# A hybrid attention and mLSTM layer: the gm gate projection moved between two stages, with longer chain steps and other buffer counts

## The chip, the cores and the metric

The kernel runs on one core of a Trainium2 chip, in one launch. The metric is the device time in microseconds. One profiled execution of the kernel before gives the trace from which all rows below come.

## The reference, cut to what matters

A layer has 2048 tokens of 1024 features behind 16 learned meta tokens. One input projection feeds two branches and four gates, and all of it is float32:

```python
u = _rmsnorm(h, norm_pre[layer])
proj = u @ w_in
(a_q, a_k, a_v, a_z, m_qk, m_v, m_i, m_f, m_o, m_z, g_a, g_m) = jnp.split(proj, SPLIT_POINTS, axis=-1)
att = _swa_sink_branch(a_q, a_k, a_v, sinks)      # window 128, sinks, partial rotary
y_a = (att * silu(a_z)) @ w_attn_out
m_q, m_k = split(silu(_causal_conv(m_qk, conv_w, conv_b)))
cell = _mlstm_cell(m_q, m_k, m_v, m_i, m_f)       # matrix memory, chunkwise
hm = _head_layernorm(sigmoid(m_o) * cell, head_norm)
y_m = (hm * silu(m_z)) @ w_mlstm_out
merged = sigmoid(g_a) * y_a + sigmoid(g_m) * y_m
out = h + _rmsnorm(merged @ w_out, norm_post)     # meta tokens dropped
```

The projection that the change moves is the last 1024 columns of `w_in`, those of `g_m`.

## The kernel before, in words

Each float32 operand of a matmul is split into a high and a low part of type float32r, and a product is three matmuls (high by high, high by low, low by high) that add up in one PSUM bank.

**The main stage** handles the tokens in two halves of 1024 (8 blocks of 128). In each half it goes through `PLAN`, four groups, one for each kv head and each mLSTM head. A group has an A block (`kind == "A"`: q, k and v of one kv head, 8 token tiles of 384 columns), an F block (`kind == "F"`: q and k of one mLSTM head, 4 feature tiles of 512 tokens) and an M block (`kind == "M"`: v and output gate of one mLSTM head, 8 token tiles of 512 columns). Behind the M blocks of groups 1 and 3 stands one more F block, a gate block: four feature tiles of `ga` for two token blocks of 512, 8 tiles. Every tile is 24 matmuls (8 slices of the contraction by 3), in `token_proj` or `feat_proj`. The second half repeats the plan.

TensorE's order is the order of the program; the other engines' instructions are ordered by the framework's own planner. To fill TensorE while a chain waits for other engines, the program is cut into **slots**. After every 6 matmuls of a projection, and once after every tile, `slot()` runs: a tile has 4 slots. A chain is a Python generator that puts out one step of its instructions and then yields how many slots must pass before the next step. An attention chain (`attn_block`) of a token block and kv head has five steps, separated by `ATT_YIELDS`: transposes of q and k; scores and exponentials of two heads; those of the other two and the normalised P; transposes of P, masks (`pc`, `pp`, `pmb`); the product with V (`acc`). An mLSTM chain (`mlstm_chain`) has three, separated by `ML_YIELDS`, and starts right behind its M tile.

Attention chains wait in `queue`. `slot()` starts one when `clock[0]` reaches `clock[1]` and `clock[0] % SLOTS == CHAIN_PHASE`, and the next at least `gap[0]` slots later: 12, or 8 for the last group of the second half. Buffers such as `qkv` (8) and `vt` (10) limit how many blocks may be on their way, so each tile of an A block is preceded by

```python
while len(queue) > HALF_BLOCKS - 1 - i or done[0] < total - HALF_BLOCKS + i:
    slot()
```

which runs slots without a projection between them. At the end of the stage `drain(True)` runs slots in the same way until the last chain has ended. `load_w` fetches the weights of a block in 8 slices into staging tiles (`wraw` and `wraw2`) and splits them on ScalarE (high) and VectorE (low) into `whi` and `wlo`. A gate tile leaves through `evict_f`: a tanh on ScalarE and a store to HBM.

Besides, `weight_sums` and `token_sums` build the sums of quarter matrices that the second stage needs, by DMAs from ScalarE's queue (copies) and POOL's queue (adding transfers), one every fifth slot from slot 80 on.

**The second stage** does six 1024x1024 products, az, mz, gm, att, hm and out (`MATS`), for each half of the tokens: 12 sets. A set replaces the eight products of quarter matrices by seven (`PRODS`), each of 48 matmuls of 512 columns: 336 for a set. `SETS` orders them: az, mz and gm of the first half, the same of the second half, then att, hm and out with both halves each. For each product `fetch` loads its operands, `prep` splits them (`split`, lines 963 and 964) and the matmuls of line 1142 run. Products P1 and P2 of a set begin with fresh banks. The operands `r` stay resident over sets with the same key (the tokens' operands for az, mz and gm of a half; the weights for both halves of att, hm and out): only the first set of a key loads and splits two operands per product, the others one. A finished quarter leaves through `quarter`: az and mz with a load, a tanh, several VectorE operations and stores of the operands of the later sets (`operands`), gm with one tanh and one store, hm with two loads. Loads and stores share SyncE's queue.

## Time and profile before

| | us |
|---|---|
| runs shown | 2470.49 and 2477.13, median 2473.81 |
| the profiled execution | 2478.5 |
| its span, first to last instruction | 2476.8 |
| main stage, to the last matmul of a projection | 0 to 1490 |
| second stage | 1490 to 2477 |

The profiled execution lies 4.7 us above the median. Its busy times are TensorE's matmuls 2309.2 us, weight loads 1946.3, VectorE 1591.3, ScalarE 1109.9 and POOL 595.0. A busy share over the whole span mixes both stages; the windows below part them, and each window gives the granted clock as a mean, where 1.00 is 2.4 GHz and 0.50 would be 1.2 GHz throughout.

### The profile page before, as it was taken

How to read it: one execution, taken by the hardware profiler on the slowest of the kernel's cores; microseconds unless marked ns; L12 is line 12 of the kernel's file. 1: busy time of each engine (PE TensorE's matmuls, PEld its weight loads, DVE VectorE, ACT ScalarE, POOL GpSimd, SP SyncE). 2: the span in 40 equal slices, each digit the busy share in tenths (PEclk: the TensorE clock that was granted, in tenths of full speed). 3: DMA queues.
4: the chain of work that ended last, by engine and by line, in shares of the span. 5: the costliest groups of instructions: out<-in, count | busy, mean ns of one | idle time of the engine just before them, and what ended most of it. 6: DMA issues, size and time to landing. Idle time of an engine off the chain costs nothing.

```text
span 2476.8 us, 34095 instructions
## 1 busy us (share of the span) xinstructions
PE 2309.2 (93%) x11149; PEld 1946.3 (79%) x11149; DVE 1591.3 (64%) x3435; ACT 1109.9 (45%) x2721; POOL 595.0 (24%) x1219
## 2 busy tenths in 40 slices
PE   7997899897998898999998998999999999989897
PEld 7786689787787787789887886788878888877685
DVE  7875664574766675764776855764587363666675
ACT  6543543453455454553554544434533442323442
POOL 5243344234342435434343430000000000000010
PEclk9998999998999998999999999999999999999998
DMA  6424456534567536545311118876797676889874
GB/s 227 131 54 123 113 106 117 154 91 99 124 157 226 154 103 110 123 109 130 93 47 48 47 52 269 283 223 212 234 297 229 212 252 218 286 269 305 283 262 140
DMA packets 216916, 415.53 MB, mean 168 GB/s; under 512 B 23212, under 2 KB 80896, under 8 KB 216736
## 3 DMA queue, kind: packets, MB, share of 16 engines
q1 hardware_dynamic: 200032, 352.51, 43.8%
q0 software_dynamic: 9792, 35.66, 9.9%
q10 hardware_dynamic: 6912, 25.17, 3.4%
q8 instruction: 88, 1.44, 0.2%
q14 instruction: 92, 0.75, 0.1%
HBM read 302.06 MB, written 172.00 MB: 191 GB/s over the span
## 4 chain that ended last, share of the span: by engine, by line
PE 38%; DVE 12%; DMA 10%; ACT 4%; issue 3%; POOL 2%; SPq 0%; ACTq 0%; DVEq 0%; POOLq 0%
PE x L1142 21%; PE pj L754 8%; PE pj L766 4%; DMA raw<-uo_d 3%; PE acc L519 2%; DVE xs L531 1%; DMA ld<-gm_d 1%; DVE st L964 1%; DMA wraw<-in_w_all 1%; DMA raw<-sw_d 1%; DVE r L964 1%; DVE wlo L213 1%; DVE e L1083 1%; PE s L467 1%; ACT r L963 1%
## 5 line engine op out<-in xcount | busy, mean ns | idle before, releaser
L1142 PE MATMUL x<-r,st 128*128 128x512 f32 x2688 | 623.0, 394 | 29.2 <-DVE st L964 9.5
L754 PE MATMUL pj<-whi,un 128*128 128x512 f32 (+2 forms) x1952 | 628.6, 379 | 0.1
L1142 PEld LDWEIGHTS x<-r,st 128*128 128x128 f32 x2688 | 512.2, 191 | 139.8 <-DVE st L964 10.9
L754 PEld LDWEIGHTS pj<-whi,un 128*128 128x128 f32 x1952 | 373.3, 193 | 39.7 <-issue 1.3
L754 PE MATMUL pj<-wlo,un 128*128 128x512 f32 (+2 forms) x976 | 365.2, 374 | 12.0 <-DVE wlo L213 12.0
L964 DVE TENSOR_TENSOR st<-raw,st 128x1024 fp32r<-128x1024 f32 x168 | 204.4, 1220 | 201.8 <-ACT st L963 194.4
L766 PE MATMUL pj<-un,whi 128*128 128x512 f32 x1024 | 327.7, 401 | 2.7 <-ACT xs L542 2.7
L1142 PE MATMUL x<-st,r 128*128 128x512 f32 x1344 | 309.2, 392 | 9.2 <-DVE st L964 5.3
L963 ACT CAST st<-raw 128x1024 fp32r<-128x1024 f32 x168 | 176.6, 1052 | 292.6 <-PE x L1142 158.8
L1142 PEld LDWEIGHTS x<-st,r 128*128 128x128 f32 x1344 | 253.8, 189 | 64.4 <-DVE st L964 6.0
L1050 POOL TENSOR_TENSOR yss<-yss,mhalf 128x1 f32<-128x1 f32 x16 | 12.6, 797 | 971.2 <-issue 895.2
L766 PEld LDWEIGHTS pj<-un,whi 128*128 128x128 f32 x1024 | 187.7, 191 | 38.0 <-ACT xs L542 3.1
L754 PEld LDWEIGHTS pj<-wlo,un 128*128 128x128 f32 x976 | 189.0, 194 | 34.4 <-DVE wlo L213 19.0
L766 PE MATMUL pj<-un,wlo 128*128 128x512 f32 x512 | 203.1, 397 | 0.0
L476 ACT ACTIVATE P<-s,mn 128x144 f32<-128x144 f32 x256 | 95.3, 377 | 233.2 <-DVE mn L474 200.8
L213 DVE TENSOR_TENSOR wlo<-wraw,whi 128x512 fp32r<-128x512 f32 (+3 forms) x224 | 138.7, 635 | 23.4 <-ACT whi L212 21.6
L964 DVE TENSOR_TENSOR r<-raw,r 128x1024 fp32r<-128x1024 f32 x66 | 80.5, 1222 | 96.3 <-ACT r L963 96.1
L212 ACT CAST whi<-wraw 128x512 fp32r<-128x512 f32 (+3 forms) x224 | 112.0, 530 | 41.7 <-DMA wraw<-in_w_all 27.4
L963 ACT CAST r<-raw 128x1024 fp32r<-128x1024 f32 x66 | 69.2, 1051 | 113.4 <-DMA raw<-sw_d 43.9
L766 PEld LDWEIGHTS pj<-un,wlo 128*128 128x128 f32 x512 | 97.5, 190 | 21.9
L502 POOL TENSOR_SCALAR_AFFINE_SELECT pp<-pc 128x512 fp32r<-128x512 f32 x120 | 78.7, 659 | 118.7 <-ACT pc L497 107.7
L467 PE MATMUL s<-ks,qs 128*128 128x272 f32 (+1 forms) x512 | 90.7, 298 | 15.8 <-ACT ks L448 7.5
(363 smaller groups left out, 3528.6 us busy)
## 6 DMA issues: line engine op xcount, KB each, us to landing
raw<-sw_d SPq DMA_DIRECT2D x72, 512.0 KB, 5.7
raw<-in_wq SPq DMA_DIRECT2D x54, 512.0 KB, 4.5
wraw<-in_w_all SPq DMA_DIRECT2D x96, 256.0 KB, 4.4
sw_d<-in_wq POOLq DMA_DIRECT2D x48, 512.0 KB, 7.2
raw<-uo_d SPq DMA_DIRECT2D x28, 512.0 KB, 5.4
raw<-op_att_d SPq DMA_DIRECT2D x28, 512.0 KB, 5.4
raw<-op_hm_d SPq DMA_DIRECT2D x28, 512.0 KB, 5.7
raw<-op_mg_d SPq DMA_DIRECT2D x28, 512.0 KB, 5.5
```

The source lines that it names most:

```text
L212: S.copy(hi[:, :w], raw[:, :w])
L213: tt(lo[:, :w], raw[:, :w], f(hi)[:, :w], ALU.subtract)
L467: T.matmul(sp[:, pa, c0:272], lhsT=qs[:, pr, pa, :], rhs=ks[:, i, c0:272], start=(i == 0), stop=(i == 1))
L476: S.activation(P[:, 2 * pa + pr], sp[:, pa, 128:272], AF.Exp, bias=mn[:, 2 * pr + pa:2 * pr + pa + 1], scale=-1.0, accum_out=mn[:, 4 + 2 * ...
L502: G.affine_select(pp[:, i], f(pc)[:, i], pattern=[[0, 4], [-1, 128]], compare_op=ALU.is_gt, fill=0.0, base=0, channel_multiplier=1)
L519: T.matmul(acc, lhsT=l, rhs=r.rearrange("p s q -> p (s q)"), start=(i == 0), stop=(i == len(ops) - 1))
L531: stt(acc[:, :n], raw[:, i:i + n], cw_t[:, tix, i:i + 1], acc[:, :n], ALU.mult, ALU.add)
L754: T.matmul(ps[:, :w], lhsT=us[k][:, a, o:o + 128], rhs=ww[k][:, :w], start=(n == 0), stop=(n == 3 * KT - 1))
L766: T.matmul(ps, lhsT=ww[k][:, 128 * i:128 * i + 128], rhs=us[k][:, a], start=(n == 0), stop=(n == 3 * KT - 1))
L963: S.copy(op[:, 0], raw)
L964: tt(op[:, 1], raw, f(op)[:, 0], ALU.subtract)
L1142: T.matmul(banks[bset][g], lhsT=l, rhs=r, start=(fresh and p == 0 and kk == 0 and m == 0), stop=(p == 1 and kk == 1 and m == 2), skip_grou ...
```

## The change

The matmuls of gm leave the second stage, which keeps ten sets, and come into the main stage: each half has four gate blocks, `gm` behind groups 0 and 2 and `ga` behind 1 and 3, of the same form. `gate_d["gm"]` is then written by `evict_f`. Its quarter sums fall away, and `weight_sums` takes the five matrices as two pairs and a single one. The steps of both chains stand further apart. P has two buffers, `vt` 11 instead of 10, the split weight halves 11 instead of 10, and the `wraw` staging 3 instead of 4. The `done` test of the loop is looser by one chain. The bank that takes the transposed meta part of P is no longer that of the product with V; it is a tile of its own, and `acc` is taken in the last step. The layer norm's last operation (subtract the mean, multiply) moves from VectorE to two small POOL operations and one ScalarE activation. The scratch for descriptors of POOL's DMAs is 4096 instead of 8192.

```diff
--- before.py
+++ after.py
@@ -36,8 +36,8 @@
 NHALF = NB // HALF_BLOCKS
 SBH = HALF_BLOCKS * 128 // SB
 BIG = 1e30
-ATT_YIELDS = (5, 4, 5, 5)
-ML_YIELDS = (3, 5)
+ATT_YIELDS = (5, 5, 8, 9)
+ML_YIELDS = (4, 6)
 CHAIN_PHASE = 2
 DMA_LEAD = 30
 SPLIT_LEAD = 2
@@ -76,13 +76,12 @@
         tg(i)
         fblock([("q", i), ("k", i)])
         th(i)
-        if i % 2:
-            fblock([("ga", 2 * i - 2 + j) for j in range(4)])
+        fblock([("ga" if i % 2 else "gm", 4 * (i // 2) + j) for j in range(4)])
     return plan
 
 
 PLAN = _plan()
-MATS = ("az", "mz", "gm", "att", "hm", "out")
+MATS = ("az", "mz", "att", "hm", "out")
 
 
 @with_exitstack
@@ -100,7 +99,7 @@
     dram = pool("dram", 1, DRAM)
     es1 = ExitStack()
     units = pool("units", 16, None, es1)
-    wp = pool("wp", 10, None, es1)
+    wp = pool("wp", 11, None, es1)
     stage = pool("stage", 4, None, es1)
     mconst = pool("mconst", 1, None, es1)
     ps_p = pool("ps_p", 2, PSUM, es1)
@@ -179,7 +178,7 @@
 
     def weight_sums():
         for a in range(0, len(MATS), 2):
-            pair = (a, a + 1)
+            pair = range(a, min(a + 2, len(MATS)))
             for op, i, src in ((cp, 2, (0, 0)), (cp, 0, (1, 1)), (add, 2, (0, 1)), (add, 0, (0, 1)),
                                (cp, 1, 2), (add, 1, (1, 1)), (cp, 3, 1), (add, 3, (1, 0))):
                 for m in pair:
@@ -201,7 +200,7 @@
             if seq[0] % 5 >= 3:
                 raw = extra[0].tile([128, SB], F32, name="wraw2")
             else:
-                raw = wp.tile([128, SB], F32, name="wraw", bufs=4)
+                raw = wp.tile([128, SB], F32, name="wraw", bufs=3)
             seq[0] += 1
             with (ExitStack() if first else tc.high_priority(offset=DMA_LEAD)):
                 nc.sync.dma_start(out=raw[:, :w],
@@ -427,7 +426,7 @@
             put(qkv[:, 320:384], ps[:, 256:320])
             apply_rope(qkv.rearrange("p (h d) -> p h d", d=64), b, 6, 128)
             last = b % HALF_BLOCKS == HALF_BLOCKS - 1
-            vt = vcar[g] if last and b < NB - 1 else wt("vt", [128, 2, HD], R, bufs=10)
+            vt = vcar[g] if last and b < NB - 1 else wt("vt", [128, 2, HD], R, bufs=11)
             vp = vcar[g] if b % HALF_BLOCKS == 0 else vring[0]
             vring[0] = vt
             put(vt[:, 0], ps[:, 320:384])
@@ -455,7 +454,7 @@
                 V.tensor_copy(kcar[g], f(ks)[:, :, 144:272])
             kring[0] = ks
             yield ATT_YIELDS[0]
-            P = wt("P", [128, 4, 144], bufs=1)
+            P = wt("P", [128, 4, 144], bufs=2)
             mn = wt("mn", [128, 16])
             c0 = 0 if b > 0 else 128
             for pr in range(2):
@@ -486,11 +485,10 @@
                             rv.broadcast_to([128, 2, 2, NM]), ALU.mult)
             tt(Pv[:, :, :, NM:], Pv[:, :, :, NM:], rv.broadcast_to([128, 2, 2, 128]), ALU.mult)
             yield ATT_YIELDS[2]
-            acc = ps_a.tile([128, SB], F32, name="acc")
+            tm = ps_a.tile([128, SB], F32, name="acc")
             tp = ps_t.tile([128, SB], F32, name="tr")
             for s in range(4):
                 T.transpose(out=tp[:, 128 * s:128 * s + 128], in_=P[:, s, 16:144], identity=ident_t)
-            tm = acc
             T.transpose(out=tm[0:64, 0:128], in_=Pm.rearrange("p s j -> p (s j)"), identity=ident_t)
             pc = wt("pc", [128, 2, 4, 128], R, bufs=1)
             tpv = tp.rearrange("p (s q) -> p s q", s=4)
@@ -515,6 +513,7 @@
                    (vt.rearrange("p a d -> p (a d)"), pc[:, 1])]
             if b > 0:
                 ops += [(vp.rearrange("p a d -> p (a d)"), pp[:, 0]), (vp.rearrange("p a d -> p (a d)"), pp[:, 1])]
+            acc = ps_a.tile([128, SB], F32, name="acc")
             for i, (l, r) in enumerate(ops):
                 T.matmul(acc, lhsT=l, rhs=r.rearrange("p s q -> p (s q)"), start=(i == 0), stop=(i == len(ops) - 1))
             bs = stage.tile([128, SB], F32, name="xs")[0:64]
@@ -643,7 +642,9 @@
             V.bn_aggr(sm[:, 8:10], sm[:, 2:8])
             ts(sm[:, 10:11], sm[:, 1:2], 4.0 * EPS, sm[:, 9:10], ALU.mult, ALU.add)
             G.tensor_tensor(sm[:, 11:12], sm[:, 10:11], mh_t[:, 0:1], ALU.pow)
-            ts(tho, tho, sm[:, 8:9], sm[:, 11:12], ALU.subtract, ALU.mult)
+            G.tensor_tensor(sm[:, 12:13], sm[:, 8:9], sm[:, 11:12], ALU.mult)
+            G.tensor_scalar(sm[:, 13:14], sm[:, 12:13], -1.0, 0.0, ALU.mult, ALU.add)
+            S.activation(tho, tho, AF.Identity, bias=sm[:, 13:14], scale=sm[:, 11:12])
             yield ML_YIELDS[1]
             th = ps_t.tile([128, SB], F32, name="tr")
             for i in range(2):
@@ -667,7 +668,7 @@
             rsqrt_mean(rs[:, 0], rs[:, 1], EPS)
 
         def raw_first():
-            tiles = [wt("P", [128, 4, 144], bufs=1).rearrange("p s q -> p (s q)")]
+            tiles = [wt("P", [128, 4, 144], bufs=2).rearrange("p s q -> p (s q)")]
             tiles += [wt("pmb", [128, 4, 128], bufs=1).rearrange("p s q -> p (s q)")]
             tiles += [wt("v1", [128, 2, VW], bufs=3).rearrange("p a n -> p (a n)") for _ in range(3)]
             tiles += [wt("qs", [128, 2, 2, 128], bufs=1).rearrange("p a b q -> p (a b q)")]
@@ -837,7 +838,7 @@
                     chains = []
                     for i in range(HALF_BLOCKS):
                         rs = None
-                        while len(queue) > HALF_BLOCKS - 1 - i or done[0] < total - HALF_BLOCKS + i:
+                        while len(queue) > HALF_BLOCKS - 1 - i or done[0] < total - HALF_BLOCKS + i - 1:
                             slot()
                         if c == 0 and arg == 0:
                             if i == 0:
@@ -951,7 +952,7 @@
     ring = pool("ring", 1)
     ps_1 = pool("ps_1", 4, PSUM)
     ps_0 = pool("ps_0", 4, PSUM)
-    SETS = [(n, c, ("u", c)) for c in range(NPAIR) for n in ("az", "mz", "gm")]
+    SETS = [(n, c, ("u", c)) for c in range(NPAIR) for n in ("az", "mz")]
     SETS += [(n, c, ("w", n)) for n in ("att", "hm", "out") for c in range(NPAIR)]
     OPD = {"att": "att", "hm": "hm", "out": "mg"}
     IDX = {"P1": 0, "P2": 1, "P6": 2, "P5": 3, "P7": 4, "P3": 5, "P4": 6}
@@ -1177,7 +1178,7 @@
     r["mxT"] = a["meta_tokens"].T.reshape(KT, 128, NM).transpose(1, 0, 2)
     r["gpre"] = a["norm_pre"][0].reshape(KT, 128).T
     r["w_all"] = np.concatenate([_pack(w_in, cols) for _, _, cols in PLAN])
-    mats = [w_in[:, c:c + D] for c in (C_AZ, C_MZ, C_GM)] + [a[n][0] for n in ("w_attn_out", "w_mlstm_out", "w_out")]
+    mats = [w_in[:, c:c + D] for c in (C_AZ, C_MZ)] + [a[n][0] for n in ("w_attn_out", "w_mlstm_out", "w_out")]
     r["wq"] = np.stack([m.reshape(2, 4, 128, 2, SB).transpose(0, 3, 2, 1, 4).reshape(2, 2, 128, 4 * SB) for m in mats])
     r["negs"] = a["attn_sinks"][0]
     r["cw"] = a["conv_w"][0].T.reshape(KT, 128, 4).transpose(1, 0, 2)
@@ -1204,7 +1205,7 @@
     import concourse.bacc as bacc
     from concourse.bass_utils import run_bass_kernel_spmd
 
-    nc = bacc.Bacc("TRN2", target_bir_lowering=False, num_devices=1, dynamic_dma_scratch_size=8192)
+    nc = bacc.Bacc("TRN2", target_bir_lowering=False, num_devices=1, dynamic_dma_scratch_size=4096)
     arrays, args = {}, []
     for name, a in _layout(inputs).items():
         arrays[f"in_{name}"] = a
```

## Rows read from the trace of the kernel before

**Rows 1.** The page's busy times: us, share of the span, instructions.

```profile
PE 2309.2 (93%) x11149; PEld 1946.3 (79%) x11149; DVE 1591.3 (64%) x3435; ACT 1109.9 (45%) x2721; POOL 595.0 (24%) x1219
```

**Rows 2.** Windows, both stages: length, busy by engine, clock, DMA share, GB/s.

```profile
0.00:1490.00 1490.00, 1377.42 (x7117) 1180.29 (x7117) 978.21 (x2637) 713.54 (x2178) 582.36 (x1203) 0.96 0.45 114
1490.00:2477.00 987.00, 931.79 (x4032) 765.98 (x4032) 613.10 (x798) 396.34 (x544) 12.59 (x16) 0.97 0.76 249
```

**Rows 3.** Windows: A1, A2, A3 of half 1, A1, A3 of half 2; gate block with A2.

```profile
167.00:241.00 74.00, 61.17 (x337) 56.50 (x337) 41.45 (x119) 30.17 (x117) 30.56 (x69) 0.86 0.36 104
...
401.00:445.00 44.00, 44.00 (x273) 42.77 (x272) 19.48 (x56) 17.09 (x65) 25.44 (x57) 1.00 0.50 117
548.00:622.00 74.00, 61.02 (x329) 56.23 (x328) 40.24 (x116) 28.43 (x109) 31.93 (x71) 0.86 0.43 102
928.00:992.00 64.00, 54.90 (x289) 50.45 (x288) 36.43 (x102) 26.25 (x96) 34.78 (x70) 0.87 0.66 113
...
1275.00:1335.00 60.00, 51.43 (x286) 47.70 (x285) 33.50 (x99) 25.23 (x94) 28.89 (x63) 0.94 0.10 30
...
1090.60:1183.20 92.60, 92.60 (x490) 82.91 (x490) 43.75 (x116) 36.30 (x118) 39.88 (x75) 1.00 0.56 131
```

**Rows 4.** The chain that ended last: start, length, matmuls of 384 columns.

```profile
1175.08 8.32 PE pj L754 x48
```

**Rows 5.** Windows of sets: az, mz, gm, az, gm, att, hm, out.

```profile
1498.00:1578.00 80.00, 79.36 (x336) 65.16 (x337) 55.26 (x66) 40.83 (x52) 0.00 (x0) 0.96 0.83 279
1578.00:1662.50 84.50, 79.10 (x338) 64.93 (x337) 58.77 (x83) 31.43 (x44) 0.00 (x0) 0.96 0.75 242
1662.50:1739.10 76.60, 76.47 (x338) 63.01 (x337) 39.81 (x47) 34.92 (x47) 0.00 (x0) 1.00 0.70 229
1739.10:1815.30 76.20, 76.20 (x338) 63.10 (x337) 49.58 (x62) 37.31 (x50) 0.00 (x0) 1.00 0.75 249
1898.30:1974.50 76.20, 76.20 (x337) 63.08 (x337) 40.13 (x47) 35.11 (x47) 0.00 (x0) 1.00 0.69 230
1974.50:2050.60 76.10, 76.10 (x337) 63.02 (x336) 44.08 (x50) 31.98 (x39) 0.00 (x0) 1.00 0.79 266
2204.00:2292.70 88.70, 80.31 (x338) 64.78 (x337) 64.55 (x92) 23.27 (x28) 0.00 (x0) 0.96 0.91 300
2292.70:2383.40 90.70, 80.18 (x337) 65.24 (x337) 60.71 (x82) 41.49 (x64) 2.94 (x3) 0.94 0.80 259
```

**Rows 6.** TensorE's waits, whole span: us, times, longest us.

```profile
PE acc L519 <- POOL pmb L511: 29.3, 12, 4.4
PE tr L492 <- DVE P L487: 16.8, 9, 4.6
...
PE pj L754 <- DVE wlo L213: 12.0, 13, 3.3
...
PE s L467 <- ACT P L476: 5.7, 1, 5.7
```

**Rows 7.** The same in the window 167 to 241, an A1 block.

```profile
PE acc L519 <- POOL pmb L511: 8.2, 3, 4.4
...
PE tr L492 <- DVE P L487: 1.0, 1, 1.0
```

**Rows 8.** Timeline: VectorE at the border mz to gm; TensorE in out's second product.

```profile
1670.47 0.75 DVE L1098 SCALAR_TENSOR_TENSOR bt<-ld,hn,th 128x512 f32<-128x512 f32 x1 [1.92 <-DMA op_hm_d<-bt]
...
1672.94 1.22 DVE L964 TENSOR_TENSOR st<-raw,st 128x1024 fp32r<-128x1024 f32 x1
...
2320.29 2.07 PE L1142 MATMUL x<-r,st 128*128 128x512 f32 x4 [7.34 <-DVE ld L1108]
```

**Rows 9.** VectorE's wait for POOL; POOL's small step; its transfers' time to landing.

```profile
DVE tho L646 <- POOL msm L645: 61.1, 63, 3.1
...
L645 POOL TENSOR_TENSOR msm<-msm,mhalf 128x1 f32<-128x1 f32 x64 | 37.6, 588 | 8.5 <-DVE msm L644 7.8 <-DMA kT<-in_xT 0.7
...
DMA to landing us min/median/max: 5.4/7.1/11.7
```

## The prediction, made before the change was run

> **What bounds the kernel now.** I began with the page's busy times: TensorE is busy 93% of the span, its weight loads 79%, and nothing else over 64% [rows 1]. So TensorE sets the time, and the question is which matmuls come and go and in which of its gaps. The windows by stage come next: the main stage (to 1490 us) has 112.6 us without a matmul and a granted clock of 0.96, the seven-product stage behind it 55.2 us and 0.97 [rows 2]. The change takes work out of the second and puts it into the first, so I read both by block.
>
> The main stage's lost time is not spread evenly. Its A blocks (8 token tiles of 192 matmuls in all) come in two kinds [rows 3]: A2, which follows a gate block, has no gap (44.0 us busy of 44.0), A1 and A3, which follow an M block directly, have 12.8, 13.0, 9.1 and 8.6 us of gap and a clock of 0.86 to 0.94. The code says why. A chain of attention steps may start every 12 slots and 8 are queued, 96 slots; the next A block begins 80 slots behind the last one's end if no gate block stands between, and 112 if one does. Its `while` loop then turns `slot()` with no projection beside it. Counting slots by the loops, A1 and A3 have 21, 20, 16 and 16 such bare slots, all other blocks none.
>
> In the second stage I cut the windows at each 336 matmuls, one set [rows 5]. A set without a stall takes 76.2 us. The two gm sets take 76.6 and 76.2: they are among the smooth ones. The lost time sits in mz, hm and out.
>
> **The change, part by part.** *Removed matmuls.* Two gm sets, 2 x 336, at 76.6 + 76.2: **-152.8 us** [rows 5]. With them go 28 weight loads of 512 KB, their splits, 32 tanh and 32 stores, all beside matmuls.
>
> *Added matmuls.* 4 blocks x 8 tiles x 24 = 768. Pace: 76.2/336 = 0.2268 us for 512 columns [rows 5], so **+174.2**. The Trainium skill (TensorE: Matmul & The Clock Gate, Back-to-back issue gap) gives 131 ns for such a matmul in a stream with weight loads; no row here is that fast. By it the swap would be +100.6 - 88.0 and the whole sum about 9 us lower; the row decides. The new gates' evictions, stores and weight splits are those of the ga blocks, which run without a gap (part of the 92.6 us stretch in [rows 3]), so they are hidden. If that cover failed, the nearest price is what late weight halves cost now, 12.0 us over 28 blocks [rows 6]: four more blocks, **+2** (0 to 4).
>
> *Bare slots gone.* With a gate block in every group, the same count gives 112 slots against 96 each time and, with the looser `done` test, no bare slot in any A block, although a chain grows from 19 to 27 slots. What that gives back: the 92.6 us stretch (a gate block and A2) holds 192 matmuls at 0.2268, 192 of 384 columns at 8.32/48 = 0.1733 [rows 4], and some 106 small ones in the 15.8 us left, 0.149 each [rows 3]. By these prices A1 and A3 with their x337, x329, x289 and x286 would take 54.9, 53.7, 47.8 and 47.3 us in place of 74, 74, 64 and 60 [rows 3]: **-68**. The lower bound is the gaps alone, -44; the upper is gaps plus what the lower clock takes, 0.14, 0.14, 0.13 and 0.06 of their lengths, -76. The small matmuls are not saved; they move under the gm blocks.
>
> *Longer chain steps.* They target waits of a chain on itself. TensorE waits 29.3 us for the masked block of the last step (L511), 16.8 for the normalised P, 5.7 for the exponentials of the first half [rows 6]. Of the first two, 23.8 and 6.0 are inside A1 and A3 (one of the four blocks stands in [rows 7], the others show 7.2 and 1.0, 4.2 and 2.0, 4.2 and 2.0) and are counted already. Outside them 5.5 + 10.8 + 5.7 = 22 us remain. The steps of 8 and 9 slots (before 5 and 5) add 4 us and more where the longest waits are 4.6 and 4.4; the 5.7 us one gets a single slot more, 1.4 us. I take 16 of the 22 and 4 of clock: **-20**, between 0 (the helpers' queues were late, not the step short) and -34 (all 22, and 12 of the 27 us that the lower clock takes outside A1 and A3: 0.04 x 1490 less 33). The second buffers of P, the eleventh of V and of the weight halves go with this; staging holds 11 + 3 + 2 weight tiles instead of 10 + 4 + 2, so loading looks as far ahead as before.
>
> *The layer norm's last step* moves from VectorE (27 us in all) to ScalarE behind two more POOL steps. VectorE is busy 978 of 1490 us in the main stage, ScalarE 714 [rows 2], and the step's result is used 6 slots later: 0, see the second rival.
>
> *End of the main stage.* The last group starts chains every 8 slots; the eighth now ends 5 slots after the last tile. What could be late there is L511 once, at most 4.4 us [rows 6], and five matmuls: **+3** (0 to 8). Next late behind it are the second stage's first loads.
>
> *The gm sets were also a pause.* mz is followed by gm, which loads only weights and evicts with one tanh; now az of the next half follows the first mz and att the second. Both split two operands per product instead of one. VectorE is the engine that feels it: 55.3 and 58.8 us busy in az and mz, 39.8 in gm [rows 5]. At mz to gm it waits 1.92 us for a buffer whose store has to land (1670.47), and its split for the second product comes at 1672.94, just in time [rows 8]: that border loses 0.4. Two operands put 2.4 us of splits ahead of that point and two more loads on SP's queue, behind stores that wait for VectorE. The nearest prices: az to mz loses 84.5 - 76.2 = 8.3 (busy evictions, one operand follows); hm to out 90.7 - 76.2 = 14.5 (the same evictions, two operands follow, and one 7.34 us wait for a late load [rows 5, 8]). I take 11 for each of two borders, **+22**, with ends of 1 and 29.
>
> *Weight sums.* 80 steps instead of 96, each on ACT's or POOL's queue every fifth slot, and done long before the stage ends: 0.
>
> **The sum.** Main stage 174 + 2 - 68 - 20 + 3 = +91; second stage -153 + 22 = -131; together **-40**. The profiled execution took 2478.5 us (span 2476.8), 4.7 above the median of the runs shown, so 2438 for it and **2433** on the median's scale. The ends: main stage +64 (174 + 0 - 76 - 34 + 0) and +142 (174 + 4 - 44 + 0 + 8); second stage -152 and -124; together -88 and +18. Five terms do not reach their ends at once.
>
> **The rivals.** *1. The borders cost nothing and the steps heal all.* For it: gm to az and gm to att lose nothing with two operands (76.2 and 76.1 for the sets after gm [rows 5]), so two operands alone are no load. Against: the set ahead was light there. Time: 174 + 1 - 68 - 34 + 1 - 152 = -78, 2396; anything under 2424 belongs here. Chance 0.33.
>
> *2. ScalarE waits for POOL and holds TensorE (slower).* VectorE waits for the one POOL step 61.1 us in 63 places [rows 9]. On ScalarE the wait is for three steps; at 0.59 us for each of the two new ones [rows 9] that is about 61 + 64 x 1.18 = 137 us. ScalarE empties the projection's two banks in order, so what stands behind such a wait is the next tile's eviction. If all reached TensorE: 2570. It decides against the change once 40/137, three in ten, get through; half gives 2433 + 68 = 2501. Against it: ScalarE is idle half of the stage, and each bank has a tile's time, 24 x 0.2268 = 5.4 us, of slack. Chance 0.06.
>
> *3. POOL is held by its transfers.* The scratch of its queue is halved. Its 68 transfers (60 after) issue without waiting now, and land in 7.1 us, at most 11.7 [rows 9]; they are issued five slots apart, some 6.8 us. If each had to wait for the one before, POOL would stand up to 4.9 us, on average perhaps 1; with one in two ahead of a mask that TensorE needs, 30 x 2 = +60, 2493. The Trainium skill (DMA: Bandwidth & Descriptors, SWDGE vs HWDGE vs iDMA) says that such transfers are described in rings kept in a part of SBUF; that a smaller one would stop POOL is my inference, and no row shows it. Chance 0.05.
>
> *4. The change doesn't do what it says:* the longer chains run bare slots again, and half of the 68 us stays: 2467. Against it stands the slot count. Chance 0.06.
>
> **How the numbers follow.** The forecast holds 0.50, the rivals 0.33, 0.06, 0.05 and 0.06. A range from 2398 to 2472 leaves out the deepest tenth (the low end of rival 1) and rivals 2 and 3. Two per cent, about what a measurement of this kernel can tell, is 49 us: faster 0.35 (rival 1 and an edge of the forecast), same 0.60, slower 0.05 (the larger part of rival 2).
>
> **What would show it.** Gate blocks in all eight groups of 53 to 55 us; A1 and A3 without gaps, the clock of the main stage at 0.98; L511 and P gone from the list of TensorE's waits; a main stage ending near 1580; five pairs of sets behind it, with stalls in the second product of the second half's az and of att. The forecast is wrong if the main stage grows by much else than 91, or if the borders cost under 5 or over 15 us.

## The result, and the profile after

The changed kernel took 2497.95 and 2501.55 us, median **2499.75**, against 2473.81 before: a ratio of 1.011 [1.0088, 1.0132]. It is slower, by 26 us; the forecast was 2433 and its range ended at 2472. The profiled execution took 2501.55 us (span 2499.5). Of the executions behind the traces below, kernel 12's alone ran in a slower state, at a granted clock of 0.83; only a count is read from it.

The page's busy times show almost nothing of this. TensorE has the same 93%:

```profile
PE 2325.8 (93%) x11245; PEld 1963.1 (79%) x11245; DVE 1548.0 (62%) x3351; ACT 1110.6 (44%) x2765; POOL 615.5 (25%) x1339
```

The windows by stage do (columns as in [rows 2]):

```profile
0.00:1650.30 1650.30, 1540.32 (x7881) 1319.90 (x7882) 982.41 (x2603) 773.91 (x2304) 602.87 (x1323) 0.97 0.41 108
1650.30:2499.50 849.20, 785.53 (x3366) 643.24 (x3364) 565.56 (x748) 336.68 (x461) 12.64 (x16) 0.96 0.79 262
```

The second stage did what was forecast. Its first matmul comes 11.8 us behind the last projection (8.6 before: +3, as forecast), and from there to the end it takes 837.4 us instead of 978.6: -141, where -131 was forecast. The main stage grew by 160.7 us (last projection at 1489.6 before, 1650.3 now), where +91 with the handover was forecast. The whole miss is in the main stage.

Note the time without a matmul there: 112.6 us before, 1650.30 - 1540.32 = 110.0 now. The bare slots are gone, and yet TensorE stands idle as long as it did. By block (windows of gm in group 0 and the A1 behind it; of the M block of group 3 and the ga block behind it, all of half 1):

```profile
164.00:216.80 52.80, 52.80 (x260) 44.04 (x258) 23.28 (x67) 20.23 (x63) 15.86 (x30) 1.00 0.37 105
216.80:261.60 44.80, 44.80 (x278) 43.12 (x277) 22.54 (x58) 16.22 (x63) 26.01 (x56) 1.00 0.52 103
711.70:797.00 85.30, 71.02 (x362) 58.56 (x362) 52.69 (x155) 40.76 (x122) 28.99 (x65) 0.92 0.46 110
797.00:860.50 63.50, 56.66 (x263) 46.83 (x263) 31.68 (x80) 26.52 (x73) 17.70 (x30) 0.92 0.77 221
```

The first two rows are what the forecast described: a gate block and an A block without a gap at full clock (A1 took 74.00 us in [rows 3]). The last two are where the time went: 14.3 and 6.8 us of gap in two blocks, with the clock at 0.92. Cut at the first matmul of each block, the lengths add up so, in us:

| blocks | before | after | change | forecast |
|---|---|---|---|---|
| gm (4, new) | 0 | 223 | +223 | +174 |
| A1 and A3 | 273 | 168 | -104 | -68 |
| both together | 273 | 391 | +119 | +106 |
| M | 576 | 600 | +24 | |
| ga | 220 | 231 | +11 | |
| F | 222 | 227 | +5 | |
| A0 and A2 | 193 | 196 | +2 | |
| M, ga, F, A0, A2 together | 1212 | 1254 | +42 | -20 |

TensorE's waits (columns as in [rows 6]):

```profile
PE tr L612 <- DVE pc L496: 26.6, 19, 7.2
PE x L1143 <- DVE st L965: 18.8, 5, 5.8
...
PE tr L555 <- DVE xs L272: 9.2, 3, 5.5
...
PE tr L586 <- DVE mn L477: 6.8, 3, 2.5
PE tr L612 <- DVE ks L448: 6.4, 6, 3.8
...
PE acc L518 <- POOL pmb L509: 2.1, 1, 2.1
```

The masked block of the last step, 29.3 us in [rows 6], is down to 2.1, and P's 16.8 is off the list: that much the longer steps did. At the head of the list now stands line 612, the transpose of k with which an mLSTM chain begins. It waits for VectorE's `pc`, the copy of P's transposes out of their bank. Both tiles come from the same pool of two PSUM banks. With its other releasers line 612 waits 40.3 us in all; before, as line 613, it waited 6.6. And on ScalarE, where [rows 9] has VectorE:

```profile
ACT tho L647 <- POOL msm L646: 105.6, 62, 3.2
```

In the second stage the borders stand in az of the second half and att of the first; att of the second half, behind them, has no stall (columns as in [rows 5]):

```profile
1824.50:1910.30 85.80, 79.17 (x337) 64.90 (x336) 64.27 (x83) 40.22 (x53) 0.00 (x0) 0.94 0.86 282
...
1995.40:2078.90 83.50, 78.37 (x338) 64.06 (x337) 59.31 (x72) 34.44 (x42) 0.00 (x0) 0.96 0.90 301
...
2078.90:2155.10 76.20, 76.20 (x338) 63.10 (x337) 37.29 (x46) 25.50 (x30) 0.00 (x0) 1.00 0.71 240
```

The two borders cost 85.8 - 76.2 = 9.6 and 83.5 - 76.2 = 7.3 us, together 17 where 22 was forecast, and the timeline of TensorE has them at the second product, held by a split on VectorE:

```profile
1842.42 67.81 PE L1143 MATMUL x<-r,st 128*128 128x512 f32 x286 [6.63 <-DVE r L965]
...
2010.27 0.80 PE L1143 MATMUL x<-st,r 128*128 128x512 f32 x1 [3.66 <-DVE st L965]
2012.54 66.70 PE L1143 MATMUL x<-st,r 128*128 128x512 f32 x287 [1.48 <-DVE r L965]
```

### The profile page after: what moved, and what is told of

Same layout as the page of the kernel before. It is cut to its first block, busy times and chain, and to the rows that moved or that the text cites. A ratio compares the mean times of both kernels' runs of the same rounds, so it can differ in the third digit from the quotient of the medians.

```text
span 2499.5 us, 34409 instructions
## 1 busy us (share of the span) xinstructions
PE 2325.8 (93%) x11245; PEld 1963.1 (79%) x11245; DVE 1548.0 (62%) x3351; ACT 1110.6 (44%) x2765; POOL 615.5 (25%) x1339
## 4 chain that ended last, share of the span: by engine, by line
PE 38%; DVE 10%; DMA 9%; issue 3%; ACT 3%; POOL 1%; SPq 0%; DVEq 0%; ACTq 0%; POOLq 0%
PE x L1143 15%; PE pj L767 9%; PE pj L755 9%; DMA raw<-uo_d 3%; PE acc L518 2%; DVE st L965 1%; PE s L466 1%; DMA raw<-sw_d 1%; DVE r L965 1%; DMA ld<-part_d 1%; DVE e L1084 1%; DVE th L1094 1%; DMA ld<-gm_d 1%; ACT r L964 1%; DMA raw<-in_wq 1%
## 5 line engine op out<-in xcount | busy, mean ns | idle before, releaser
L1143 PE MATMUL x<-r,st 128*128 128x512 f32 x2016 | 473.9, 398 | 38.1 <-ACT st L964 10.6
L767 PE MATMUL pj<-un,whi 128*128 128x512 f32 x1536 | 495.1, 404 | 2.0 <-ACT xs L541 2.0
L1143 PEld LDWEIGHTS x<-r,st 128*128 128x128 f32 x2016 | 387.7, 193 | 124.0 <-DVE st L965 11.7
L767 PEld LDWEIGHTS pj<-un,whi 128*128 128x128 f32 x1536 | 286.2, 193 | 56.9 <-ACT xs L541 2.4
L767 PE MATMUL pj<-un,wlo 128*128 128x512 f32 x768 | 306.4, 399 | 0.0
L964 ACT CAST st<-raw 128x1024 fp32r<-128x1024 f32 x140 | 147.0, 1051 | 254.9 <-PE x L1143 106.2
L965 DVE TENSOR_TENSOR st<-raw,st 128x1024 fp32r<-128x1024 f32 x140 | 170.2, 1222 | 139.3 <-ACT st L964 137.2
L212 DVE TENSOR_TENSOR wlo<-wraw,whi 128x512 fp32r<-128x512 f32 (+3 forms) x256 | 171.1, 689 | 46.6 <-ACT whi L211 44.4
L767 PEld LDWEIGHTS pj<-un,wlo 128*128 128x128 f32 x768 | 147.7, 192 | 33.2
L468 DVE COPY_PREDICATED s<-um,s 128x256 f32<-128x256 int32 x120 | 50.9, 424 | 138.8 <-PE s L466 137.9
L965 DVE TENSOR_TENSOR r<-raw,r 128x1024 fp32r<-128x1024 f32 x66 | 80.4, 1223 | 73.0 <-ACT r L964 71.6
```

The costliest lines, as they stand in the source:

```text
L212: tt(lo[:, :w], raw[:, :w], f(hi)[:, :w], ALU.subtract)
L468: V.copy_predicated(sp[:, :, 144:272], um_t.rearrange("p (a t) -> p a t", a=1).broadcast_to([128, 2, 128]), sp[:, :, 0:128] if b > 0 else ...
L767: T.matmul(ps, lhsT=ww[k][:, 128 * i:128 * i + 128], rhs=us[k][:, a], start=(n == 0), stop=(n == 3 * KT - 1))
L964: S.copy(op[:, 0], raw)
L965: tt(op[:, 1], raw, f(op)[:, 0], ALU.subtract)
L1143: T.matmul(banks[bset][g], lhsT=l, rhs=r, start=(fresh and p == 0 and kk == 0 and m == 0), stop=(p == 1 and kk == 1 and m == 2), skip_grou ...
```

## The experiments

Four theories stood at the start. **A**: chains and projection tiles fall together wrongly, since `CHAIN_PHASE = 2` now holds in every group, and the k transpose meets a taken bank. **B**: ScalarE waits for POOL in the norm and holds back what TensorE needs (rival 2). **C**: the longer steps themselves. **D**: POOL is held by the smaller scratch (rival 3). Ratios are to the kernel before, timed on the same chip; its medians there were 2471.9 to 2476.7 us, so times of different pairs compare to within 5 us.

**1. The phase alone.** The changed kernel, with

```diff
-CHAIN_PHASE = 2
+CHAIN_PHASE = 1
```

> The changed kernel with attention chains starting at phase 1 of a tile's four slots instead of 2, nothing else. Theory A (banks): with no bare slots the chains keep one phase to the tiles, and in the M blocks 21 slots ask for three of the two transpose banks (one of P's transposes, two of mLSTM steps); at phase 1 the same count gives none. A expects 2455 to 2475 us, and under 3 us of waits of the k transpose (L612) for pc instead of 26.6. Theory B (ScalarE waits for POOL in the layer norm), theory C (the steps are too long) and theory D (POOL's smaller scratch) expect 2492 to 2508.

Measured: 2489.26 us, 1.0053 [1.0033, 1.0073]. Line 612's wait for `pc` halves (13.6 us, 9 times), where A expected under 3, and its wait for `ks` rises to 17.9. The time lies between the two ranges: A has a share, 10 us here.

**2. The steps alone.** The changed kernel, with

```diff
-ATT_YIELDS = (5, 5, 8, 9)
-ML_YIELDS = (4, 6)
+ATT_YIELDS = (5, 4, 5, 5)
+ML_YIELDS = (3, 5)
```

> The changed kernel with the step distances of before (5,4,5,5 and 3,5), all else as changed. Theory C expects the 20 us of gain and more back: 2440 to 2465 us. Theory A counts 17 slots with three takers of the two banks instead of 21, so 2485 to 2502. B and D expect 2492 to 2508.

Measured: 2478.67 us, 1.0023 [1.0009, 1.0038]: 21 us better with the short steps, which no theory had in its range. Line 612 still waits 26.5 us for `pc`, 18 times, so that wait does not come from the longer steps.

**3. The norm alone.** The changed kernel, with the old last operation of the layer norm:

```diff
-            G.tensor_tensor(sm[:, 12:13], sm[:, 8:9], sm[:, 11:12], ALU.mult)
-            G.tensor_scalar(sm[:, 13:14], sm[:, 12:13], -1.0, 0.0, ALU.mult, ALU.add)
-            S.activation(tho, tho, AF.Identity, bias=sm[:, 13:14], scale=sm[:, 11:12])
+            ts(tho, tho, sm[:, 8:9], sm[:, 11:12], ALU.subtract, ALU.mult)
```

> The changed kernel with the layer norm's last operation back on VectorE behind one POOL step. Theory B: ScalarE's 105.6 us of waits for POOL go, and 2440 to 2480 us come. Theories A, C and D: 2492 to 2508, with the waits for banks in the M blocks as they are.

Measured: 2479.99 us, 1.0029 [1.0013, 1.0045]: 20 us better. Line 612 still waits 19 times for `pc`, but shorter:

```profile
PE tr L612 <- DVE pc L496: 18.1, 19, 1.6
```

The longest falls from 7.2 to 1.6 us, but that one was not the wait for POOL: in the changed kernel `pc` stood on ScalarE behind a weight split whose load had not landed (ScalarE's timeline, changed kernel):

```profile
794.67 0.52 ACT L211 CAST whi<-wraw 128x392 fp32r<-128x392 f32 x1 [5.91 <-DMA wraw<-in_w_all]
795.10 0.58 ACT L495 CAST pc<-tr 128x512 fp32r<-128x512 f32 x1
```

The kernel before, with the norm on VectorE, has the same wait of ScalarE there (5.98 us), kernel 3 none above 0.95; whether the norm has a part in the late load is not shown. In one queue whatever makes ScalarE wait is paid by all that stands behind it. How the norm does it is left to kernel 15.

**4. The scratch alone.** The changed kernel, with the larger scratch (and ten buffers of weight halves, for room):

```diff
-    wp = pool("wp", 11, None, es1)
+    wp = pool("wp", 10, None, es1)
-    nc = bacc.Bacc("TRN2", target_bir_lowering=False, num_devices=1, dynamic_dma_scratch_size=4096)
+    nc = bacc.Bacc("TRN2", target_bir_lowering=False, num_devices=1, dynamic_dma_scratch_size=8192)
```

> The changed kernel with the scratch for POOL's transfers back at 8192, and 10 instead of 11 split weight halves to make room. Theory D: 2460 to 2490 us. A, B and C: 2494 to 2508, with up to 4 us for the buffer given up.

Measured: 2503.04 us, 1.0112 [1.0095, 1.013], no better than the changed kernel. D, which expected 2460 to 2490, falls.

**5. gm alone.** The kernel before with only the move of gm (`_plan`, `MATS`, the range of `pair`, `SETS`, `mats`); steps, norm, buffers, test and scratch stay old.

```diff
-        if i % 2:
-            fblock([("ga", 2 * i - 2 + j) for j in range(4)])
+        fblock([("ga" if i % 2 else "gm", 4 * (i // 2) + j) for j in range(4)])
...
-    SETS = [(n, c, ("u", c)) for c in range(NPAIR) for n in ("az", "mz", "gm")]
+    SETS = [(n, c, ("u", c)) for c in range(NPAIR) for n in ("az", "mz")]
```

> The kernel before with the gm projection moved and nothing else: steps, buffers, done test, layer norm and scratch stay as before. Theory S (the move gives what the forecast says without its 20 us for the steps, and the edits that came with it cost the rest): 2445 to 2462 us. Theory M (the move itself lengthens the blocks around it, since the bare slots were time in which the helpers caught up): 2474 to 2495.

Measured: 2469.0 us, 0.9985 [0.997, 1.0], between the ranges of the two theories. TensorE's waits in it:

```profile
PE tr L612 <- ACT tho L650: 22.9, 17, 2.2
...
PE pj L753 <- DVE wlo L212: 18.1, 14, 2.8
```

**6. All but gm.** The changed kernel with the same lines turned back, so that gm is in the second stage.

```diff
-        fblock([("ga" if i % 2 else "gm", 4 * (i // 2) + j) for j in range(4)])
+        if i % 2:
+            fblock([("ga", 2 * i - 2 + j) for j in range(4)])
...
```

> The changed kernel with gm back in the second stage: steps, buffers, done test, layer norm and scratch as changed. Theory S: 2495 to 2520 us, 20 for each of steps and norm on top of before, and perhaps more for longer chains run bare. Theory M: 2470 to 2490.

Measured: 2471.16 us, 0.9986 [0.9968, 1.0004]. Either half of the change alone costs nothing, and both together 26 us. That does not yet say that the halves collide. In kernel 6 A1 and A3 take 240.4 us instead of 272.7, and M and ga 824.6 instead of 796.1: a gain where the bare slots stand (the gaps there are 27 us instead of 43; the looser `done` test is the likely edit, not tried alone) hides a loss elsewhere. With gm moved these blocks have next to no gap, so those 32 us have no place to be won again.

**7 and 8. Norm and steps old, at phase 2 and at phase 1.** The changed kernel with the edits of 2 and 3; the second of the pair with that of 1 besides.

```diff
-ATT_YIELDS = (5, 5, 8, 9)
-ML_YIELDS = (4, 6)
-CHAIN_PHASE = 2
+ATT_YIELDS = (5, 4, 5, 5)
+ML_YIELDS = (3, 5)
+CHAIN_PHASE = 1
```

> The changed kernel with the layer norm back on VectorE and the step distances of before. If the 21 us of each add up: 2452 to 2464 us. If both cure the same waits: 2470 to 2480.

> As the run before it, with the chains' phase at 1 instead of 2. The count of slots with three takers of the two transpose banks falls from 17 to 0. If those are worth what phase 1 gave alone: 10 us below the run before it, 2442 to 2456 us where that is 2452 to 2464. If the phase only shifts waits about: within 5 us of it.

Measured: 2473.45 us, 0.9981 [0.9966, 0.9996], and 2451.0, 0.9904 [0.9885, 0.9922]. With the norm and the steps old, one slot of phase is worth 22 us.

**9. gm alone at phase 1.** Kernel 5 with the edit of 1.

```diff
-CHAIN_PHASE = 2
+CHAIN_PHASE = 1
```

> The kernel before with the gm projection moved and the chains' phase at 1 instead of 2, nothing else. Theory A (banks): the count of slots with three takers of the two transpose banks is 17 at phase 2, which is the number of TensorE's waits at the k transpose (L612) for the older step's copy with gm alone, and 0 at phase 1; so those waits go and 2442 to 2456 us come. If phase 1 helped only together with the other buffers: 2464 to 2474.

Measured: 2446.66 us, 0.9881 [0.9855, 0.9906]; the main stage ends at 1592.7 instead of 1614.1. The timelines of TensorE (start, length; only the matmuls that fill a bank of that pool with P, tho and k are shown) have the mechanism. Kernel 5, in half 2's M block of group 1:

```profile
1127.05 0.63 PE L491 MATMUL tr<-ident,P 128*128 128x128 f32 x4
...
1127.68 0.44 PE L649 MATMUL tr<-ident,tho 128*128 128x128 f32 x2
1129.34 0.33 PE L612 MATMUL tr<-ident,kT 128*128 128x128 f32 x1 [1.22 <-ACT tho L650]
```

Kernel 9, in the same block:

```profile
1120.33 0.60 PE L491 MATMUL tr<-ident,P 128*128 128x128 f32 x4
...
1123.33 0.38 PE L649 MATMUL tr<-ident,tho 128*128 128x128 f32 x2
1123.55 0.27 PE L612 MATMUL tr<-ident,kT 128*128 128x128 f32 x1
```

In the first, three takers of two banks would come within 1.1 us (1129.34 - 1.22 - 1127.05), and the third stands 1.22 us. In the second the P transposes come 3 us ahead, and nobody stands.

**10 and 11. The two missing corners.** The changed kernel at phase 1 with the norm on VectorE and the new steps, and with the norm on ScalarE and the old steps.

```diff
-CHAIN_PHASE = 2
+CHAIN_PHASE = 1
...
-            S.activation(tho, tho, AF.Identity, bias=sm[:, 13:14], scale=sm[:, 11:12])
+            ts(tho, tho, sm[:, 8:9], sm[:, 11:12], ALU.subtract, ALU.mult)
```

> The changed kernel at phase 1 with the layer norm on VectorE, so the step distances alone differ from the run of norm, steps and phase (2451 us). If the longer steps cost time by themselves: 2462 to 2480. If they only cost by their collisions at phase 2: 2446 to 2456. If they gain what the forecast said: 2425 to 2440.

```diff
-ATT_YIELDS = (5, 5, 8, 9)
-ML_YIELDS = (4, 6)
-CHAIN_PHASE = 2
+ATT_YIELDS = (5, 4, 5, 5)
+ML_YIELDS = (3, 5)
+CHAIN_PHASE = 1
```

> The changed kernel at phase 1 with the old steps, so only the place of the layer norm differs from the run of norm, steps and phase (2451 us). If ScalarE's waits for POOL cost by themselves: 2462 to 2478. If only together with collisions: 2446 to 2458.

Measured: 2454.73 us, 0.9904 [0.987, 0.9938], and 2473.79, 0.9999 [0.9981, 1.0018]. All eight corners of the changed kernel, in us:

| | new steps, norm on ScalarE | new steps, VectorE | old steps, ScalarE | old steps, VectorE |
|---|---|---|---|---|
| phase 2 | 2499.75 | 2479.99 | 2478.67 | 2473.45 |
| phase 1 | 2489.26 | 2454.73 | 2473.79 | 2451.0 |

The norm on VectorE gives 20, 5, 35 and 23 us; phase 1 gives 10, 25, 5 and 22; the old steps give 21, 7, 15 and 4. With the norm and the phase in order, the new steps are worth nothing either way: +4 by the medians, 0 by the ratios (0.9904 for kernels 8 and 10). These two kernels differ in the steps alone. What TensorE waits for in kernel 8, and in kernel 10 in place of `pmb` and P:

```profile
PE tr L491 <- DVE P L486: 12.3, 3, 5.3
...
PE acc L518 <- POOL pmb L509: 7.9, 2, 4.5
...
PE tr L410 <- POOL xs L283: 3.6, 1, 3.6
...
PE tr L612 <- DVE ks L448: 2.1, 1, 2.1
```

```profile
PE tr L612 <- DVE ks L448: 17.8, 3, 8.0
...
PE tr L410 <- POOL xs L283: 10.6, 4, 3.9
```

**12. Was the kernel before spared by its bare slots?** It had 21, 20, 16 and 16 of them, and 21 is no multiple of a tile's four slots, so they also shift the chains against the tiles. This kernel is the one before, with bare slots added until the clock is back on a tile's start: 15 more.

```diff
-                        while len(queue) > HALF_BLOCKS - 1 - i or done[0] < total - HALF_BLOCKS + i:
+                        while (len(queue) > HALF_BLOCKS - 1 - i or done[0] < total - HALF_BLOCKS + i
+                               or (arg > 0 and i == HALF_BLOCKS - 1 and clock[0] % SLOTS)):
```

> The kernel before, with its loop ahead of the last tile of A1 and A3 running on to a multiple of four slots: 15 more bare slots in all, and the chains back in the phase that they had before the first bare slots. Theory A: 17 three-taker slots instead of 2, so some 17 waits of the k transpose (L613) for the older step's copy, M blocks 15 to 25 us longer in all, and with up to 14 us for the bare slots 2485 to 2512 us. If the phase doesn't matter: M blocks within 5 us of before and 2474 to 2489.

Measured: 2512.98 us, 1.0144 [1.0112, 1.0175], 41 us slower than the kernel before and 1 us above A's range. The count:

```profile
PE tr L613 <- ACT tho L651: 16.5, 17, 1.8
```

Seventeen waits, as in kernel 5; the kernel before has 2, of 2.5 us. How the 41 us divide between the 15 slots and the waits this run does not part.

**13 and 14. gm alone at phases 0 and 3.** I had counted, slot by slot, when three takers of that pool meet: 17 times at phase 2, never at phase 1, 2 times in the kernel before. That had come out right, so the count was put to the test at the two other phases (kernel 5 with `CHAIN_PHASE` 0 and 3).

```diff
-CHAIN_PHASE = 2
+CHAIN_PHASE = 3
```

> The kernel before with gm moved, chains at phase 0. The count gives 17 slots with three takers of the two transpose banks, this time a chain's first transposes with two mLSTM steps. Theory A (the number of three-taker slots sets the loss): 2462 to 2485 us, as phase 2 (2469) and some 17 waits of the k transpose (L612). If phase 2 was bad for another reason (P's transposes falling late, say): 2442 to 2456.

> The kernel before with gm moved, chains at phase 3. The count gives 0 slots with three takers. Theory A: 2440 to 2456 us, as phase 1 (2446.7), with no group of 17 waits. If phase 1 was good for another reason: 2462 to 2480.

Measured: 2443.05 us, 0.9867 [0.9839, 0.9894], and 2441.76, 0.9867 [0.9839, 0.9896]. That the number of meetings sets the loss fails at both. At phase 0, where the count said 17 (the first transposes of a chain with two mLSTM steps), 17 waits are there, at line 439, the transposes of q and k, behind tho's and k's; but they cost 4.1 us in all. At phase 3, where it said 0, line 612 has 17 waits, and the kernel is as fast as any. TensorE's waits at phase 0:

```profile
PE tr L612 <- DVE cst L635: 11.2, 11, 1.9
...
PE pj L753 <- DVE wlo L212: 6.7, 9, 1.3
...
PE tr L439 <- ACT tho L650: 4.1, 17, 0.5
...
PE tr L612 <- ACT tho L650: 1.3, 1, 1.3
```

and at phase 3, with two of the seventeen on the timeline:

```profile
PE tr L612 <- ACT tho L650: 14.5, 17, 2.9
...
PE pj L753 <- DVE wlo L212: 1.1, 4, 0.3
```

```profile
1112.46 0.49 PE L439 MATMUL tr<-ident,qkv 128*128 128x128 f32 x3
1114.19 0.38 PE L649 MATMUL tr<-ident,tho 128*128 128x128 f32 x2
1115.09 0.33 PE L612 MATMUL tr<-ident,kT 128*128 128x128 f32 x1 [0.52 <-ACT tho L650]
1116.87 0.60 PE L491 MATMUL tr<-ident,P 128*128 128x128 f32 x4
```

At phase 3 it is the transposes of q and k that meet tho and k, not those of P, and the wait is 0.52 us instead of 1.22. And a second wait goes with the phase: the low weight halves, which VectorE splits, are late by 18.1 us at phase 2 and by 6.3, 6.7 and 1.1 at phases 1, 0 and 3. The two together are the price in the M blocks, as the gaps of those eight blocks show. They sum to 58.8 us at phase 2 and to 23.2, 29.9 and 32.4 at phases 1, 0 and 3: 35.6, 28.9 and 26.4 less. Line 612's waits for tho and those for the low halves are 41.0 us at phase 2 and 6.3, 8.0 and 15.6 there: 34.7, 33.0 and 25.4 less. (At phase 0 the wait for `cst`, 6.9 us at phase 2, takes 4.3 of it back, and line 439 its 4.1.) Outside the M blocks the gaps grow by 19, 13 and 8 us, so the main stage ends only 21, 22 and 18 us earlier than at phase 2 in these traces.

**15. Work or wait on ScalarE?** Kernel 11 with operands for the activation that are there from the start. It leaves the layer norm's mean and spread out of the output.

```diff
-            S.activation(tho, tho, AF.Identity, bias=sm[:, 13:14], scale=sm[:, 11:12])
+            S.activation(tho, tho, AF.Identity, bias=mh_t[:, 0:1], scale=mh_t[:, 0:1])
```

> The run of old steps, phase 1 and norm on ScalarE (2473.8 us), but the activation takes its scale and bias from a constant, so that the norm's mean and spread don't reach the output; the POOL operations stay and nothing on ScalarE waits for them. If the wait for POOL is the price: 2445 to 2456. If it is ScalarE's and POOL's own added work: 2468 to 2480.

Measured: 2437.31 us, 0.9856 [0.9835, 0.9876], below even the lower range: 36 us better than kernel 11 and 14 better than kernel 8, where VectorE does the work and waits for POOL. ScalarE's wait for POOL, 104.2 us in kernel 11, is gone. The added activation costs nothing; the wait is the price. The windows of the main stage, of kernel 11 and of this one, say how it arrives:

```profile
0.00:1626.53 1626.53, 1540.44 (x7885) 1317.25 (x7885) 962.52 (x2605) 782.86 (x2306) 616.36 (x1323) 0.97 0.42 110
```

```profile
0.00:1594.43 1594.43, 1522.83 (x7885) 1311.22 (x7885) 967.32 (x2605) 784.66 (x2306) 610.36 (x1323) 0.97 0.43 112
```

Of 32.1 us, 14.5 are gaps (86.1 against 71.6), and the same 7885 matmuls are busy 17.6 us longer; clock and stalls too short to be a gap are not parted there. Kernel 2 has the clearest single case of how it arrives: ScalarE stands for POOL's result, the split `dws` of an mLSTM chain stands behind that in its queue, and TensorE waits for the split (ScalarE's and TensorE's timelines of kernel 2):

```profile
951.93 0.60 ACT L647 ACTIVATE tho<-tho,msm 128x256 f32<-128x256 f32 x1 [2.10 <-POOL msm L646]
...
952.70 0.39 ACT L626 CAST dws<-dw 128x256 fp32r<-128x256 f32 x1
```

```profile
953.14 0.85 PE L586 MATMUL acc<-cs,dws 128*128 128x258 f32 x3 [2.78 <-ACT dws L626]
```

**16 and 17. The activation later, at phase 1 and at phase 3.** Kernel 11 with the activation in a step of its own, three slots after POOL's two operations.

```diff
-ML_YIELDS = (3, 5)
+ML_YIELDS = (3, 3, 2)
...
+            yield ML_YIELDS[1]
             S.activation(tho, tho, AF.Identity, bias=sm[:, 13:14], scale=sm[:, 11:12])
-            yield ML_YIELDS[1]
+            yield ML_YIELDS[2]
```

> The run of old steps, phase 1 and norm on ScalarE (2473.8 us), with the activation put into a step of its own three slots behind the POOL operations, and the transposes two slots behind that: the whole computation, the same operations and the same distance from statistics to transposes. If the price of the norm on ScalarE is the wait in its queue: 2437 to 2455 us, near the run without the wait (2437.3) and at most as long as with the norm on VectorE (2451.0). If the order in the queue doesn't change with the place in the program: 2466 to 2478.

> The run before it at phase 3. With gm alone phases 0, 1 and 3 gave 2443, 2447 and 2442 us and phase 2 alone 2469, so the phase should matter little here: within 8 us of the run before it. If waits of the k transpose (L612) for older steps come back as they did at phase 3 with gm alone (17 waits, 14.5 us): 5 to 12 us longer.

Measured: 2468.57 us, 0.998 [0.9963, 0.9997], and 2447.3, 0.9909 [0.988, 0.9938]. ScalarE's waits for POOL in the first, and in the second:

```profile
ACT tho L648 <- POOL msm L646: 100.1, 60, 5.7
```

```profile
ACT tho L648 <- POOL msm L646: 56.8, 56, 2.4
```

At phase 1 the later place in the program changes little for ScalarE (104.2 to 100.1 us): the planner puts the activation at much the same place in ScalarE's queue, in both traces 1.5 us (median) behind VectorE's last small step of the norm. At phase 3 the wait is nearly halved, and the two kernels that were expected within 8 us of each other are 21 apart. Even so the norm on ScalarE gains nothing: 2447.3 there against 2441.8 with gm alone (on different chips, 0.9909 against 0.9867, with overlapping intervals).

## Why the prediction was wrong

**The swap of matmuls and the bare slots: right.** gm blocks, A1 and A3 together came to +119 where +106 was forecast, with no gap in A1 and at most 1.0 in A3. (Not every gate block took the 53 to 55 us that were named; the eight took 52.8 to 63.5.) The pace held: the smooth att set is 76.2 us for 336 matmuls, 0.227 each. By the Trainium skill (TensorE: Matmul & The Clock Gate, Back-to-back issue gap), with 131 ns a matmul, the swap would have been 9 us better, an estimate from that figure; no row after the change comes near it.

**The second stage: right.** -141 for -131. The borders cost 9.6 and 7.3 for 11 each, at the place that was named, and rival 1, for which they were free, falls.

**The scratch and the buffers of weight halves: right at nothing.** Kernel 4 is no faster than the changed kernel: rival 3 falls. The Trainium skill (DMA: Bandwidth & Descriptors, SWDGE vs HWDGE vs iDMA) keeps the descriptors of such transfers in rings in a part of SBUF; what a smaller part costs, no run here shows. The buffers, the `done` test, the tile of its own for P's meta part and the scratch, all together, are what parts kernel 7 from 5 and 8 from 9: 0.9981 against 0.9985, and 0.9904 against 0.9881, with overlapping intervals. (The weight sums were not tried alone.) Rival 4 falls too: A1 and A3 have next to no gap.

**The longer chain steps, -20: the step that failed.** Outside gm, A1 and A3 the main stage grew by 42 us where it should have lost 20. The waits that the steps aimed at did go (29.3 + 16.8 us to 2.1 + 0), and gave nothing: put back, the old steps gained 4 to 21 us by the medians. Two things came in their place. First, when a chain no longer stands at its last step, another wait is late next. From kernel 8 to kernel 10 the waits for P and `pmb` fall by 20.2 us and those for `ks` and `xs` rise by 22.7. Of 22 us of waits I counted 16 as won and set no next wait against them; in this corner, where nothing else is wrong, the term is 0 to +4.

Second, a cost that had no term at all: **the phase**. I read the bare slots only as lost time. They also moved the chains against the tiles, and with a gate block in every group all groups stand at phase 2, where P's transposes, tho's and k's want two banks at once and the low weight halves come late. The cost against phase 1 (with gm alone against 0 and 3 too) is 22 to 27 us where the norm stays on VectorE (kernel 5 against 9, 13 and 14, 7 against 8, 3 against 10) and 5 to 10 where it does not (2 against 11, the changed kernel against 1). With the norm on ScalarE phase 1 is itself not the best: kernel 17 is 21 us below kernel 16. That the kernel before was spared by its bare slots agrees with kernel 12.

**The norm's last step, 0: failed too.** It costs 5 to 35 us by the corners, 20 in the changed kernel. Rival 2 had the wait and nearly its size: ScalarE waits 105.6 us where about 137 was estimated, and 20/105.6, a fifth, reaches TensorE. That its 2501 us for a half lies on the measured time is luck: the steps and the phase made up the rest. I gave it 0.06 on the ground that each projection bank has 5.4 us of slack. But the projection's banks are not all that ScalarE serves: a split inside a chain (`dws` in kernel 2) stands behind the same wait, and TensorE stood 2.78 us for it. Kernel 15 shows that it is the wait and not the work.

**The sum.** On the profiled executions: forecast 2438, measured 2501.5, 63 too low. M, F, ga, A0 and A2 make 62 of it, gm with A1 and A3 13, the second stage and handover -10; less the 2 us forecast for late weight halves, which are part of the blocks' lengths. By the corners, from the changed kernel to kernel 8, the norm gives 20, the phase 25 and the steps 4; with the 20 us that the steps were to give, that is 69 where the medians miss by 67. (In another order the parts differ.) With gm alone, away from phase 2, the forecast without the steps' -20 (2453) would have been 6 to 11 us too high (2446.7, 2443.1, 2441.8). Its parts fit as well: in kernel 14 gm with A1 and A3 is +113 (forecast +106), the second stage -138 (-131). So the move itself was rightly priced, and the rest of the change took it away twice over.

**What stays open.** Why VectorE's weight splits are late at phase 2 and not at the others was not traced further; nor why the count of slots had the number of meetings right at phases 0, 1 and 2 and wrong at phase 3; nor why a meeting costs so much more at phase 2 (22.9 us for 17) than at phase 0 (4.1).

**The version to keep** is the smallest: gm moved, everything else old, `CHAIN_PHASE` at 0 or 3: 0.9867 of the kernel before, 1.3% faster and some 2.3% faster than the changed kernel. Phase 1, at 0.9881, is not parted from it by the intervals.

## What to carry to other kernels

Idle slots in a hand-written interleave are two things, lost time and an offset: before counting them as won, work out where every chain then falls against the tiles, and sweep the phase again after every edit that changes a group's number of slots. A wait seen in the trace is worth at most the distance to the next late wait, and where several chains share few banks that distance can be nothing. Moving a small operation to an engine with idle time is not free when its operand comes late from another engine: here ScalarE's queue stood still for it, and what stood behind counted, not the busy share.

## What the runs showed that I had not expected

- The number of waits says little about their price: 17 waits for the copy of tho cost 22.9 us at phase 2, 14.5 at phase 3 and, at line 439, 4.1 at phase 0; the kernels of phases 2 and 3 are 27 us apart.
- ScalarE stood 105.6 us for three chained POOL operations on 128x1 elements, in 62 places, 1.7 us each; a place three slots later in the program (kernel 16) left 100.1 of kernel 11's 104.2.
- A stall can cost more than its length: the M block of group 3 with 14.3 us of gap (half 1, changed kernel) ran at a granted clock of 0.92. TensorE stood idle for 2.2 us of its first ten (711.7 to 722); the next ten ran at 0.50, 1.2 GHz, and hold 20 matmuls where the ten after, at 1.00, hold 50. But the M block of group 2, with 7.9 us of gap, ran at 1.00 throughout: the length of the gaps alone does not tell.
- Halving the scratch for POOL's descriptors changed nothing (2499.75 us, and 2503.04 with the old scratch and one weight buffer fewer).
